# Splitting the weights of two projections ahead of their use, in the feed-forward layers, and loading them back as parts

## The chip, the cores and the metric

The kernel runs on one core of a Trainium2 chip. TensorE (PE) multiplies, VectorE (DVE), ScalarE (ACT) and GpSimd (POOL) do the element-wise work, and SyncE (SP) issues nearly all DMAs, in order, on one queue that the core's 16 DMA engines serve. The metric is the device time of one execution in microseconds (us).

## What is computed

Two decoder blocks, one after the other, on 512 tokens of width 1024, in fp32. Cut to the order of the large products:

```python
# first block
h = h + s5_mixer(rmsnorm(h), ...)            # ends in y @ w_glu
h = h + square(relu(rmsnorm(h) @ w_up[0])) @ w_down[0]
h = h + sigmoid(rmsnorm(h) @ w_ple_gate[0]) * (p[0] @ w_ple_proj[0])
k, v = rope((rmsnorm(h) * kv_norm) @ w_k), (rmsnorm(h) * kv_norm) @ w_v
h = h + window_attention(rope(rmsnorm(h) * norm_mix @ w_q), k, v) @ w_o
h = h + square(relu(rmsnorm(h) @ w_up[1])) @ w_down[1]
h = h + sigmoid(rmsnorm(h) @ w_ple_gate[1]) * (p[1] @ w_ple_proj[1])
# second block: a scan layer, then a differential attention
z, x, B, C, dt = split(rms_norm(h) @ a_w_in)  # 6144 + 32 columns
x, B, C = silu(causal_conv(x, B, C))          # 4 taps
x = h + (norm(scan(x, dt, B, C) * silu(z)) @ a_w_out)
...
```

A product keeps fp32 accuracy with three passes: each operand is split exactly into a high and a low part (hi = the value rounded to the multiplier's format, lo = the rest), and hi·hi, hi·lo and lo·hi are added in PSUM.

## The kernel before

`plan` (L665) lists all weight matrices in their order of use. `Weights` (L62 to L119) streams them. A unit is one DMA of 1 MB (a few are smaller) from DRAM into one of three `raw` buffers (`load_to`, L84). A chunk of eight 128-row K tiles by 128 columns, 1024 elements per partition, is then split (`split_to`, L92): for weights with a norm's gain GpSimd multiplies the raw chunk by it in place (L100); ScalarE copies it, rounded, to `whi` (L103); VectorE or GpSimd subtracts to get `wlo` (L104). There are four `whi` and four `wlo` buffers, and `take` (L115) asks for the split two chunks ahead of the use. `lo_eng` chooses who subtracts: GpSimd in the first attention (L1135) and in the scan layer (L1398), VectorE elsewhere.

`gemm` (L721) makes one output tile of 128 features by 512 tokens at a time: 24 products for each chunk of eight K tiles (`three`, L211). The stages, in the order of time: the first mixer, `glu` (L858), the first feed-forward layer (`mlp`, L886), the gated side input (`ple`, L966), `first_attention` (L983), the second `mlp` and `ple`, `mamba` (the scan layer, L1168), `second_attention`. In `mlp` each half has 16 tiles up (`up`, L901: relu and square on ScalarE, the square once more on GpSimd, the low part on VectorE) and 8 tiles down of 16 K tiles each (`down`, L911).

In `mamba` eight groups of four tiles (B, C and two of x) and 16 gate tiles z run through `gemm`. Between them the convolution `conv` (L1262, three multiply-adds on VectorE), and the scan `ssd` (L1277) as a generator whose steps are put behind the tiles: decays `dec` are loaded by DMA from the DRAM row `acs` (L1325), get an offset on VectorE (L184), an exponential on ScalarE and a mask on GpSimd (L174).

What runs in which order on each engine is set by a scheduler that is given the program and its dependencies; within an engine, and in SP's queue, the order is then fixed, and an instruction that waits holds up those behind it.

Of the kernel before, what the change touches and what calls it, by code (L numbers as in the profile page):

```python
# [62 lines left out]
class Weights:  # L63
    """Streams the weight matrices in their order of use: DRAM -> raw fp32 -> exact (hi, lo) f32r pairs."""

    def __init__(self, nc, raw_pool, hl_pool, ahead_dma, ahead_split):
        self.nc, self.raw_pool, self.hl_pool = nc, raw_pool, hl_pool
        self.units, self.chunks = [], []
        self.loaded, self.split, self.used = 0, 0, 0
        self.ahead_dma, self.ahead_split = ahead_dma, ahead_split  # L70
        self.raw, self.hl = {}, {}
        self.lo_eng = nc.vector

    def add(self, w, k0, kt, c0, cols, cut=128, kg=8, gain=None):
# [3 lines left out]
        self.units.append((w[k0:k0 + 128 * kt, c0:c0 + cols].rearrange("(k p) n -> p k n", p=128), kt, cols))  # L78
        gain = None if gain is None else (gain, k0 // 128)
        new = [(u, k, min(kg, kt - k), c, min(cut, cols - c), gain) for c in range(0, cols, cut) for k in range(0, kt, kg)]  # L80
        self.chunks.extend(new)
        return new

    def load_to(self, u):  # L84
        while self.loaded < min(u, len(self.units)):
            ap, kt, cols = self.units[self.loaded]
# [5 lines left out]
    def split_to(self, n):  # L92
        while self.split < min(n, len(self.chunks)):
            u, k, kn, c, cn, gain = self.chunks[self.split]
            self.load_to(u + self.ahead_dma)
            src = self.raw[u][:, k:k + kn, c:c + cn]
# [11 lines left out]
    def borrow(self, shape):  # L108
        """One of the raw buffers for something else, until its last use."""
# [12 lines left out]
class Builder:  # L122
    #: the order of the queries' and gates' tiles in the second attention
    QG = (0, 1, 8, 2, 9, 3, 10, 4, 11, 5, 12, 6, 13, 7, 14, 15)
    #: the number of the queries' tiles before the values in the first attention
    V_AT = 2
    #: the groups after whose tensors the gates of groups 0, 1, ... come; those of the other groups come last
# [72 lines left out]
    def pair(self, src, g=None, name="x"):  # L200
        """src (fp32) -> exact f32r pair of src * g."""
# [14 lines left out]
    def dexp(self, out, x, n, pool):  # L216
        t = lambda nm: pool.tile([128, n], F32, tag="ex" + nm, name="ex" + nm)  # noqa: E731
# [15 lines left out]
    def dsincos(self, so, co, x, n, pool):  # L233
        t = lambda nm: pool.tile([128, n], F32, tag="sc" + nm, name="sc" + nm, bufs=1)  # noqa: E731
# [44 lines left out]
    def s5(self, extra):  # L279
        """extra: steps of work for TensorE that needs nothing of this."""  # L280
        nc, ins, tc = self.nc, self.ins, self.tc
        V, A, G = self.V, self.A, self.G
        with ExitStack() as cx:
            sm = cx.enter_context(tc.tile_pool(name="s5s", bufs=1))
            s2 = cx.enter_context(tc.tile_pool(name="s5t", bufs=2))
            small = lambda nm, n=32: sm.tile([128, n], F32, name=nm)  # noqa: E731
# [12 lines left out]
            b3 = lambda t: t.rearrange("p (r h) -> p r h", h=16)  # noqa: E731  # L299
# [15 lines left out]
            # tiles whose other blocks stay zero, for every other four pairs of groups  # L315
            two = lambda nm, sh: [sm.tile(sh, F32, name=f"{nm}{i}") for i in range(2)]  # noqa: E731
# [21 lines left out]
            # discretisation  # L338
# [75 lines left out]
            # powers of the phase of a  # L414
# [12 lines left out]
            # 1 / rms of the tokens  # L427
# [7 lines left out]
            # C, states on partitions  # L435
# [10 lines left out]
            # g*d over the channels  # L446
# [1263 lines left out]
```

## Time and profile before

| what | value |
|---|---|
| median of three runs | 2049.87 us (2049.61 to 2052.82) |
| span of the profiled execution, first to last instruction | 2043.2 us |
| what the median run takes beyond that span | 6.7 us |
| PE busy | 1919.8 us (94%) |
| DVE, ACT, POOL busy | 1271.6, 922.7, 640.8 us |
| read from HBM, written | 166.00 MB, 2.16 MB |

The page gives the profiled execution by its span alone; the runs' times lie 6.4 to 9.6 us above it. Busy time is that of instructions; issuing a DMA, waiting and branching are not counted. PEclk is the clock that TensorE was granted as a share of its full 2.4 GHz (1.00 is 2.4, half is 1.2). A row of the chain of waits gives what the chain's end was waiting for in that stretch. Records of matmuls overlap, since they are pipelined: their pace is read from how many start in a stretch.

### The profile page before, as it was taken

The page shows a single profiled execution, that of the slowest core. Times are in us where ns is not written, and L with a number is a line of the kernel's source. Part 1 is how long each engine was busy: PE and PEld are TensorE (multiplying, and loading weights), DVE is VectorE, ACT ScalarE, POOL GpSimd, SP SyncE. Part 2 cuts the span into 40 slices and gives each one's busy share as a digit, 9 for nine tenths or more (in the row PEclk, how much of TensorE's full clock was granted, in tenths as well). Part 3 has the DMA queues.
Part 4 walks back from the last instruction along what each step waited for, and adds up shares of the span by engine and source line. Part 5 has one row for each costly group of instructions (what it writes and reads, how often), then busy time and mean ns, then how long its engine had stood idle before and what let it go on. Part 6 is the DMA issues. An engine that isn't in the chain of part 4 may idle for free.

```text
span 2043.2 us, 25227 instructions
## 1 busy us (share of the span) xinstructions
PE 1919.8 (94%) x9482; PEld 1581.2 (77%) x9482; DVE 1271.6 (62%) x2042; ACT 922.7 (45%) x1590; POOL 640.8 (31%) x415
## 2 busy tenths in 40 slices
PE   3799999999999899999999999988989899999998
PEld 1688888888887787888888886766867678887888
DVE  8995543333448685633333457988888764727885
ACT  5644333223334376442233335456656643434553
POOL 7500122012117720231022117456655543432000
PEclk9899999999999899999999999988999899999999
DMA  5003323323322431333323313232323223425331
GB/s 137 6 7 117 103 83 103 102 85 102 103 95 81 125 95 53 96 91 103 102 85 101 103 54 105 69 98 88 98 72 103 87 74 117 119 88 138 111 93 42
DMA packets 232059, 185.78 MB, mean 91 GB/s; under 512 B 22611, under 2 KB 213790, under 8 KB 231938
## 3 DMA queue, kind: packets, MB, share of 16 engines
q1 hardware_dynamic: 219072, 179.43, 29.8%
q10 hardware_dynamic: 12866, 4.75, 0.9%
q8 instruction: 75, 1.23, 0.2%
q14 instruction: 46, 0.38, 0.1%
HBM read 166.00 MB, written 2.16 MB: 82 GB/s over the span
## 4 chain that ended last, share of the span: by engine, by line
PE 68%; DVE 18%; ACT 5%; issue 4%; POOL 2%; DMA 2%; SPq 0%; ACTq 0%; DVEq 0%; POOLq 0%
PE pg L190 62%; DVE cy L177 3%; DVE lent L171 2%; DVE dec L184 1%; PE pm L190 1%; PE sc L190 1%; ACT L187 1%; DVE wlo L104 1%; DVE pr L182 1%; ACT whi L103 1%; DMA dec<-acs 1%; DVE h L171 1%; PE po L190 1%; DVE xl L177 1%; PE o L190 1%
## 5 line engine op out<-in xcount | busy, mean ns | idle before, releaser
L103 ACT ACTIVATE whi<-raw 128x1024 fp32r<-128x1024 f32 x289 | 304.4, 1055 | 691.7 <-PE pg L190 601.7
L190 PE MATMUL pg<-xh,whi 128*128 128x512 f32 x1424 | 567.7, 399 | 8.3 <-ACT xh L187 4.8
L190 PE MATMUL pg<-xl,whi 128*128 128x512 f32 x1424 | 563.3, 396 | 2.2 <-DVE xl L171 2.2
L190 PE MATMUL pg<-xh,wlo 128*128 128x512 f32 x1424 | 562.7, 395 | 0.0
L104 DVE TENSOR_TENSOR wlo<-raw,whi 128x1024 fp32r<-128x1024 f32 (+1 forms) x229 | 300.3, 1314 | 367.7 <-ACT whi L103 367.5
L190 PEld LDWEIGHTS pg<-xh,whi 128*128 128x128 f32 x1424 | 271.1, 190 | 68.5 <-ACT xh L187 5.6
L190 PEld LDWEIGHTS pg<-xl,whi 128*128 128x128 f32 x1424 | 271.3, 191 | 62.9 <-DVE xl L171 4.5
L190 PEld LDWEIGHTS pg<-xh,wlo 128*128 128x128 f32 x1424 | 271.0, 190 | 57.3 <-issue 1.6
L174 POOL TENSOR_TENSOR b<-a 128x512 f32<-128x512 f32 x64 | 98.9, 1545 | 438.2 <-ACT a L187 418.7
L190 PE MATMUL pg<-hh,whi 128*128 128x512 f32 x512 | 199.2, 389 | 0.0
L190 PE MATMUL pg<-hl,whi 128*128 128x512 f32 x512 | 199.2, 389 | 0.0
L190 PE MATMUL pg<-hh,wlo 128*128 128x512 f32 x512 | 199.2, 389 | 0.0
L104 POOL TENSOR_TENSOR wlo<-raw,whi 128x1024 fp32r<-128x1024 f32 x60 | 157.2, 2623 | 110.0 <-ACT whi L103 109.5
L171 POOL TENSOR_TENSOR acc<-acc,sq 128x512 f32<-128x512 f32 x48 | 75.9, 1588 | 314.6 <-ACT sq L187 276.3
L100 POOL TENSOR_TENSOR raw<-raw,gv 128x1024 f32<-128x1024 f32 x44 | 93.6, 2146 | 139.8 <-DMA raw<-in_b_w_in_dram 54.8
L177 DVE SCALAR_TENSOR_TENSOR cy<-cx,cw,cy 128x511 f32<-128x511 f32 (+2 forms) x96 | 107.4, 1134 | 9.5 <-ACT cy L187 9.1
L190 PEld LDWEIGHTS pg<-hh,wlo 128*128 128x128 f32 x512 | 96.1, 188 | 20.0
L190 PEld LDWEIGHTS pg<-hh,whi 128*128 128x128 f32 x512 | 96.1, 188 | 20.0
L190 PEld LDWEIGHTS pg<-hl,whi 128*128 128x128 f32 x512 | 96.1, 188 | 19.9
L171 DVE TENSOR_TENSOR t<-pg,r 128x512 f32<-128x512 f32 x48 | 32.7, 688 | 107.5 <-PE pg L190 107.4
L187 ACT ACT_TABLE_LOAD x61 | 78.3, 1283 | 34.4 <-DVE cy L177 19.4
L171 DVE TENSOR_TENSOR hl<-b,hh 128x512 fp32r<-128x512 f32 x64 | 44.2, 691 | 56.9 <-POOL b L174 56.9
(409 smaller groups left out, 3132.8 us busy)
## 6 DMA issues: line engine op xcount, KB each, us to landing
raw<-in_w_up_dram SPq DMA_DIRECT2D x32, 1024.0 KB
raw<-in_w_down_dram SPq DMA_DIRECT2D x32, 1024.0 KB
raw<-in_a_w_in_dram SPq DMA_DIRECT2D x16, 1024.0 KB
raw<-in_ssm_w_glu_dram SPq DMA_DIRECT2D x8, 1024.0 KB
raw<-in_w_ple_gate_dram SPq DMA_DIRECT2D x8, 1024.0 KB
raw<-in_a_w_in_dram SPq DMA_DIRECT2D x16, 512.0 KB
dec<-acs SPq DMA_DIRECT2D x32, 256.0 KB
raw<-in_a_w_out_dram SPq DMA_DIRECT2D x8, 1024.0 KB
```

The costliest lines, as they stand in the source:

```text
L100: self.nc.gpsimd.tensor_tensor(out=src, in0=src, in1=g, op=MUL)
L103: self.nc.scalar.activation(out=hi, in_=src, func=ACTF.Copy)
L104: self.lo_eng.tensor_tensor(out=lo, in0=src, in1=hi.bitcast(F32), op=SUB)
L171: (eng or self.V).tensor_tensor(out=out, in0=a, in1=b, op=op)
L174: self.G.tensor_tensor(out=out, in0=a, in1=b, op=op)
L177: self.V.scalar_tensor_tensor(out=out, in0=a, scalar=s, in1=b, op0=op0, op1=op1)
L182: eng.tensor_scalar(out=out, in0=a, scalar1=s1, scalar2=None, op0=op0)
L184: eng.tensor_scalar(out=out, in0=a, scalar1=s1, scalar2=s2, op0=op0, op1=op1)
L187: self.A.activation(out=out, in_=in_, func=func, **kw)
L190: self.T.matmul(out=out, lhsT=lhsT, rhs=rhs, start=start, stop=stop)
```

## The change

The weights `w_k`, `w_v` and `w_q` of the first attention (12 chunks) and all columns of `a_w_in` in the scan layer but the 32 of dt (48 chunks) are marked `early`. They have no unit in the `raw` buffers any more. Their split is done in half chunks (512 elements per partition), one in each `up` tile of the two feed-forward layers and two in each `down` tile of them (but for the last two of the second half): 60 in each layer, 120 in all. A step stores the two parts of the half chunk before the last in DRAM, loads the next raw half chunk, and splits the one that was loaded a step ago: the gain (first attention's only) on GpSimd, the high part on ScalarE, the low part on VectorE in place. Raw halves have two buffers and high parts two. At the place of use `split_to` now issues two DMAs, of 512 KB each, from DRAM into `whi` and `wlo`; nothing is split there.

```diff
+    def early_step(self, more=True):
+
+        nc, pool = self.nc, self.early_pool
+        if self.done:
+            (chunk, h), raw, hi = self.done
...
+            nc.sync.dma_start(out=self.kept[chunk][h, 0], in_=hi.bitcast(F32))
+            nc.sync.dma_start(out=self.kept[chunk][h, 1], in_=raw)
+            self.done = None
+        was, self.came = self.came, None
+        if more and self.n_early < len(self.early):
...
+            raw = pool.tile([128, 512], F32, tag="eraw", name="eraw", bufs=2)
+            nc.sync.dma_start(out=raw.rearrange("p (k n) -> p k n", k=n),
+                              in_=self.units[u][0][:, k + h * n:k + h * n + n, c:c + cn])
+            self.came = (chunk, h), raw
+        if was:
...
+                nc.gpsimd.tensor_tensor(out=x, in0=x, in1=g, op=MUL)
+            hi = pool.tile([128, 512], F32R, tag="ehi", name="ehi", bufs=2)
+            nc.scalar.activation(out=hi, in_=raw, func=ACTF.Copy)
+            nc.vector.tensor_tensor(out=raw.bitcast(F32R), in0=raw, in1=hi.bitcast(F32), op=SUB)
+            self.done = (*was, hi)
...
     def split_to(self, n):
...
+            if self.units[u][3]:
+                hi = self.hl_pool.tile([128, kn, cn], F32R, tag="whi", name="whi")
+                lo = self.hl_pool.tile([128, kn, cn], F32R, tag="wlo", name="wlo")
+                for i, t in enumerate((hi, lo)):
+                    self.nc.sync.dma_start(out=t.rearrange("p k n -> p (k n)").bitcast(F32).rearrange("p (h n) -> p h n", h=2),
+                                           in_=self.kept[chunk][:, i].rearrange("h p n -> p h n"))
...
             def up(m, ps):
...
+                self.W.early_step()
...
             def down(m, ps):
...
+                    if m == 6:
+                        self.W.early_end()
+                if hf == 0 or m < 6:
+                    for _ in range(2):
+                        self.W.early_step()
```

In `plan` the units of `w_k`, `w_v`, `w_q` and of `a_w_in` (but the first, of 32 columns) get `early=True`. The line numbers of the kernel after are higher by 57 to 67 than those of before.

GpSimd in the scan layer, over one group's scan; `wlo` are the low parts of weights, `dec` the decays, `cy` the tensors of the group. Before:

```order
L174 TENSOR_TENSOR dec_10640<-dec_10640,cb_10556 128x512
L174 TENSOR_TENSOR dec_10641<-dec_10641,cb_10556 128x512
L104 TENSOR_TENSOR wlo<-raw,whi 128x1024
L174 TENSOR_TENSOR dec_10714<-dec_10714,cb_10556 128x512
L174 TENSOR_TENSOR dec_10715<-dec_10715,cb_10556 128x512
L104 TENSOR_TENSOR wlo<-raw,whi 128x1024 x2
L174 TENSOR_TENSOR cy_9987<-cy_9987,r_10503 128x512
L174 TENSOR_TENSOR cy_10059<-cy_10059,r_10503 128x512
```

The same engine and place after:

```order
L231 TENSOR_TENSOR dec_11520<-dec_11520,cb_11436 128x512
L231 TENSOR_TENSOR dec_11521<-dec_11521,cb_11436 128x512
L231 TENSOR_TENSOR dec_11592<-dec_11592,cb_11436 128x512
L231 TENSOR_TENSOR dec_11593<-dec_11593,cb_11436 128x512
L231 TENSOR_TENSOR cy_10881<-cy_10881,r_11385 128x512
L231 TENSOR_TENSOR cy_10953<-cy_10953,r_11385 128x512
```

The subtractions between the scan's own instructions are gone from GpSimd, all 48 of them in this layer.

ScalarE in the tiles up of the first feed-forward layer (`a` is the relu of a tile, `hh` its square). Before:

```order
L187 ACTIVATE hh_2800<-a_2798 128x512
L103 ACTIVATE whi<-raw 128x1024
L187 ACTIVATE a_2835<-pg 128x512
L187 ACTIVATE hh_2837<-a_2835 128x512
L103 ACTIVATE whi<-raw 128x1024
```

After, where `ehi` is the high part of an early half chunk and `eraw` what its DMA brought:

```order
L160 ACTIVATE whi<-raw 128x1024
L244 ACTIVATE a_2795<-pg 128x512
L120 ACTIVATE ehi<-eraw 128x512 x2
L244 ACTIVATE hh_2797<-a_2795 128x512
L160 ACTIVATE whi<-raw 128x1024
L244 ACTIVATE a_2840<-pg 128x512
L244 ACTIVATE hh_2842<-a_2840 128x512
L120 ACTIVATE ehi<-eraw 128x512
```

The scheduler took the early splits ahead of where the program has them: the 60 of the first layer stand between the 10th and the 60th split of a streamed chunk in ScalarE's order (from `glu` on, 50 tiles in all), those of the second between the 95th and the 140th (45 tiles, from the product with `w_o` on).

SP's queue in the first feed-forward layer, tiles down: before, `raw<-in_w_down_dram` stands there eight times in a row. After:

```order
L136 DMA raw<-in_w_down_dram 128x16x128
L108 DMA eraw<-in_a_w_in_dram 128x4x128
L99 DMA kept_3723<-eraw 128x512
L98 DMA kept_3814<-ehi 128x512
L108 DMA eraw<-in_a_w_in_dram 128x4x128
L99 DMA kept_3814<-eraw 128x512
L108 DMA eraw<-in_a_w_in_dram 128x4x128
L98 DMA kept_3814<-ehi 128x512
L136 DMA raw<-in_w_down_dram 128x16x128
```

Between two loads of streamed weights there are now about seven DMAs of 256 KB each; each store waits for ScalarE or VectorE, and each load of `eraw` for the landing of the store that frees its buffer.

## Rows read from the trace of the kernel before

**Rows 1.** The page: busy time by engine, and the chain's shares by engine.

```profile
PE 1919.8 (94%) x9482; PEld 1581.2 (77%) x9482; DVE 1271.6 (62%) x2042; ACT 922.7 (45%) x1590; POOL 640.8 (31%) x415
...
PE 68%; DVE 18%; ACT 5%; issue 4%; POOL 2%; DMA 2%; SPq 0%; ACTq 0%; DVEq 0%; POOLq 0%
```

**Rows 2.** Busy time by stretch: length, engines (instructions), PEclk, DMA share, GB/s.

```profile
200.00:610.00 410.00, 410.00 (x1808) 339.12 (x1808) 168.27 (x170) 135.76 (x174) 66.63 (x45) 1.00 0.33 99
650.00:700.00 50.00, 41.09 (x193) 32.66 (x192) 40.35 (x28) 18.06 (x27) 41.18 (x21) 0.90 0.27 81
700.00:810.00 110.00, 106.79 (x718) 88.61 (x718) 78.52 (x194) 80.12 (x228) 24.71 (x13) 1.00 0.35 99
860.00:1190.00 330.00, 330.00 (x1455) 272.88 (x1455) 128.41 (x131) 107.71 (x137) 57.05 (x37) 1.00 0.33 96
1250.00:1650.00 400.00, 358.31 (x1789) 287.00 (x1790) 325.00 (x455) 233.54 (x300) 229.04 (x127) 0.93 0.29 89
```

**Rows 3.** Groups by line, 300 to 600 us: busy, mean ns, idle before, releaser.

```profile
L104 DVE TENSOR_TENSOR wlo<-raw,whi 128x1024 fp32r<-128x1024 f32 x56 | 68.5, 1223 | 113.3 <-ACT whi L103 113.3
L103 ACT ACTIVATE whi<-raw 128x1024 fp32r<-128x1024 f32 x55 | 58.4, 1061 | 199.6 <-PE pg L190 186.8 <-issue 12.8
...
L171 DVE TENSOR_TENSOR hl<-b,hh 128x512 fp32r<-128x512 f32 x26 | 18.0, 693 | 24.2 <-POOL b L174 24.2
L187 ACT ACTIVATE hh<-a 128x512 fp32r<-128x512 f32 x26 | 16.5, 633 | 1.3
```

**Rows 4.** Groups by line on DVE, 1250 to 1650 us.

```profile
L184 DVE TENSOR_SCALAR dec<-dec,tok 128x128 f32<-128x128 f32 x128 | 50.8, 458 | 8.6 <-ACT ea L187 7.7 <-issue 0.8
L177 DVE SCALAR_TENSOR_TENSOR cy<-cx,cw,cy 128x509 f32<-128x509 f32 x32 | 41.3, 1296 | 0.2
L177 DVE SCALAR_TENSOR_TENSOR cy<-cx,cw,cy 128x510 f32<-128x510 f32 x32 | 37.8, 1185 | 0.2
L177 DVE SCALAR_TENSOR_TENSOR cy<-cx,cw,cy 128x511 f32<-128x511 f32 x32 | 29.3, 919 | 9.1 <-ACT cy L187 9.1
...
L177 DVE SCALAR_TENSOR_TENSOR xl<-cy,gv,xh 128x512 fp32r<-128x512 f32 x10 | 13.0, 1310 | 8.1 <-ACT xh L187 8.1
```

**Rows 5.** The tiles dec and cy on DVE, same stretch: ns min/median/max.

```profile
L184 DVE TENSOR_SCALAR dec<-dec,tok x128: 269/279/2423, 1339.8 to 1623.5; 128x128 f32<-128x128 f32 x128
...
L177 DVE SCALAR_TENSOR_TENSOR cy<-cx,cw,cy x96: 654/745/2940, 1276.9 to 1606.4; 128x511 f32<-128x511 f32 x32, 128x510 f32<-128x510 f32 x32, 128x509 f32<-128x509 f32 x32
L177 DVE SCALAR_TENSOR_TENSOR cy<-cy,dsk,yd x16: 735/740/750, 1357.2 to 1637.3; 128x512 f32<-128x512 f32 x16
L177 DVE SCALAR_TENSOR_TENSOR xl<-cy,gv,xh x10: 739/999/2358, 1397.2 to 1564.3; 128x512 fp32r<-128x512 f32 x10
```

**Rows 6.** Groups by line on POOL, 1250 to 1650 us.

```profile
L104 POOL TENSOR_TENSOR wlo<-raw,whi 128x1024 fp32r<-128x1024 f32 x48 | 126.8, 2643 | 98.3 <-ACT whi L103 97.8 <-PE pg L190 0.5
L174 POOL TENSOR_TENSOR dec<-dec,cb 128x512 f32<-128x512 f32 x32 | 45.5, 1437 | 34.7 <-ACT dec L187 30.4 <-DVE cb L171 4.2
L174 POOL TENSOR_TENSOR cy<-cy,z 128x512 f32<-128x512 f32 x15 | 22.0, 1470 | 2.8 <-ACT z L187 2.3
L174 POOL TENSOR_TENSOR cy<-cy,ea 128x384 f32<-128x384 f32 x16 | 18.4, 1153 | 24.1 <-DVE ea L171 23.8
L174 POOL TENSOR_TENSOR cy<-cy,r 128x512 f32<-128x512 f32 x10 | 13.8, 1406 | 6.8 <-DVE r L790 6.8
```

**Rows 7.** The chain of waits, 640 to 692 us: start, us, what.

```profile
658.43 5.18 POOL raw L100 x2
...
679.90 2.90 DVE cosT L171
```

**Rows 8.** The chain of waits in the scan layer: two of its DMAs.

```profile
1355.41 7.59 DMA dec<-acs
...
1560.91 3.11 DMA dec<-acs
```

**Rows 9.** What SP's queue waited for: us in total, times, longest.

```profile
SPq L1325 <- DMA acs<-dt: 2.6, 1, 2.6
```

More of the change, by code (lines that the diff above doesn't have):

```diff
@@ L72, in __init__, with add @@
         self.lo_eng = nc.vector
-    def add(self, w, k0, kt, c0, cols, cut=128, kg=8, gain=None):
+        self.early, self.kept, self.n_early, self.came, self.done = [], {}, 0, None, None
+    def add(self, w, k0, kt, c0, cols, cut=128, kg=8, gain=None, early=False):
         u = len(self.units)
-        self.units.append((w[k0:k0 + 128 * kt, c0:c0 + cols].rearrange("(k p) n -> p k n", p=128), kt, cols))
+        self.units.append((w[k0:k0 + 128 * kt, c0:c0 + cols].rearrange("(k p) n -> p k n", p=128), kt, cols, early))
         gain = None if gain is None else (gain, k0 // 128)
@@ L81, in add, with keep, early_end @@
         self.chunks.extend(new)
-        return new
+        if early:
+            self.early.extend((x, h) for x in new for h in range(2))
+        return new
+    def keep(self, pool, dram):
+        self.early_pool, self.dram = pool, dram
+    def early_step(self, more=True):
+        nc, pool = self.nc, self.early_pool
+        if self.done:
+            (chunk, h), raw, hi = self.done
+            if chunk not in self.kept:
+                self.kept[chunk] = self.dram.tile([2, 2, 128, 512], F32, name=f"kept{len(self.kept)}")
+            nc.sync.dma_start(out=self.kept[chunk][h, 0], in_=hi.bitcast(F32))
[3 more added lines that the diff above has]
+        if more and self.n_early < len(self.early):
+            chunk, h = self.early[self.n_early]
+            self.n_early += 1
+            u, k, kn, c, cn, _ = chunk
+            n = kn // 2
+            raw = pool.tile([128, 512], F32, tag="eraw", name="eraw", bufs=2)
[3 more added lines that the diff above has]
+        if was:
+            ((u, k, kn, c, cn, gain), h), raw = was
+            if gain is not None:
+                n = kn // 2
+                o = self.gcol[gain[0]] + gain[1] + k + h * n
+                g = self.gains[:, o:o + n].unsqueeze(2).to_broadcast([128, n, cn])
+                x = raw.rearrange("p (k n) -> p k n", k=n)
+                nc.gpsimd.tensor_tensor(out=x, in0=x, in1=g, op=MUL)
[3 more added lines that the diff above has]
+            self.done = (*was, hi)
+    def early_end(self):
+        while self.done or self.came:
+            self.early_step(False)
     def load_to(self, u):
         while self.loaded < min(u, len(self.units)):
-            ap, kt, cols = self.units[self.loaded]
+            ap, kt, cols, early = self.units[self.loaded]
+            if early:
+                self.loaded += 1
+                continue
             t = self.raw_pool.tile([128, kt, cols], F32, tag="raw", name="raw")
@@ L93, in split_to @@
         while self.split < min(n, len(self.chunks)):
-            u, k, kn, c, cn, gain = self.chunks[self.split]
+            u, k, kn, c, cn, gain = chunk = self.chunks[self.split]
             self.load_to(u + self.ahead_dma)
+            if self.units[u][3]:
[4 more added lines that the diff above has]
+                                           in_=self.kept[chunk][:, i].rearrange("h p n -> p h n"))
+                self.hl[self.split] = (hi, lo)
+                self.split += 1
+                continue
             src = self.raw[u][:, k:k + kn, c:c + cn]
@@ L674, in plan @@
         self.plan_mlp_gate(0)
[L675 removed]
+        W.add(ins["w_k"], 0, 8, 0, 256, gain="kv", early=True)
         for m in range(0, 8, 2):
             if m == self.V_AT:
[L678 to L679 removed]
+                W.add(ins["w_v"], 0, 8, 0, 256, cut=256, kg=4, gain="kv", early=True)
+            W.add(ins["w_q"][0], 0, 8, m * 128, 256, gain="mix1", early=True)
         W.add(ins["w_ple_proj"][1], 0, 2, 0, D, cut=512)
@@ L927, in mlp @@
         self.drop(r2[0])
+        cx.close()
         return out, acc2
```

16 lines of the change are left out of this document (8 added, 8 removed).

## The prediction, made before the changed kernel ran

> **What bounds the kernel now.** I read the page first [rows 1]: PE is busy for 94% of the span and 68% of the chain that ended last, so only a stage in which PE waits can give much. The table by stretch [rows 2] says which stages these are. From 200 to 610 us and from 860 to 1190 us (`glu` and the two feed-forward layers) PE is busy in every microsecond at the full clock, and DVE, ACT and POOL have half their time or more left; a tile of 24 products takes 24 x 410 / 1808 = 5.44 us there. In the first attention (650 to 810 us) PE idles 8.9 + 3.2 us, and the granted clock of 0.90 in its first 50 us means 10 us at half speed, thus 5 us of work lost: 17 us in all. In the scan layer (1250 to 1650 us) PE idles 41.7 us, and the clock of 0.93 costs 0.07 x 400 = 28 us: 70 us in all. These 87 us are the most that the change can win. What PE waits for in the scan layer is mostly DVE, busy 325 of 400 us, with ACT at 234 and POOL at 229 beside it.
>
> **What leaves the scan layer.** POOL loses 48 subtractions of 2643 ns [rows 6], 127 of its 229 us. ACT loses 48 copies of 1061 ns [rows 3], 51 us. DVE loses no instruction, but much waiting: its multiply-adds of the convolution have a median of 745 ns and means of 919, 1185 and 1296 ns, with single ones of 2940 ns; the decays' offsets have a median of 279 ns and a mean of 458 ns [rows 4, 5]. The form that reads PSUM for one of its inputs (`cy<-cy,dsk,yd`) never leaves 735 to 750 ns. The long ones take about one POOL instruction more than the short ones. Over the medians this is 108.4 - 96 x 0.745 = 36.9 us for the convolution, 128 x 0.179 = 22.9 us for the decays, and 13.0 - 10 x 0.739 = 5.6 us for `xl` over its least: 65 us of DVE's 325. How much of it is due to the subtractions? If a DVE instruction that starts while POOL works waits for the rest of POOL's instruction, the share goes by count times the square of the duration: 335 for `wlo` and 66, 32, 21 and 20 for the other four [rows 6], 71%. By busy time alone it would be 127 of 229, 55%. The longest DVE instructions, 2.1 to 2.2 us over the median, exceed the mean of every other group of POOL there by half and more [rows 5, 6], which speaks for the first: 0.7 x 65 = 45 us. The Trainium skill has this as a rule (SBUF — State Buffer, "SBUF: two separate sides"): DVE and GpSimd share one pair of ports as an exclusive lock for a whole instruction, and the loser fully blocks. By it 45 us would come free, by a shared bandwidth 36 us; the trace agrees with the lock.
>
> So DVE falls from 325 to 280 us, ACT to 183, POOL to 102, for PE work of 400 - 70 = 330 us. DVE was late, then PE is. Not all 70 us come back: the chain dt, softplus, decays is serial, the same two engines still hand work to each other in a fixed order at 85% load of DVE, and the decays' DMAs now queue behind twice the bytes: 48 MB of parts instead of 24 MB. One decay load took 7.59 us behind other loads, one 3.11 us without [rows 8]; 16 pairs of loads that meet a 1 MB load 0.2 times more often lose 16 x 0.2 x 4.5 = 14 us at most if all stood on the chain, and nothing if none did. I take two thirds of the 70 us, which is also what DVE is freed of: **-45 us** (bounds -70 and -20).
>
> **What leaves the first attention.** Its 12 gains, 12 copies and 12 subtractions go. Between 658 and 666 us the chain is two gains of 2.6 us in front of the products that feed the residual, and later the product with the cosines takes 2.90 us on DVE beside POOL [rows 7], where like ones take 0.69 us [rows 3]. That is 5.2 + 2.2 = 7.4 us, and the half clock that follows such waits is 5 us [rows 2]: **-12 us** of the 17 (bounds -17 and -4).
>
> **What comes into the feed-forward layers.** Per half chunk ACT gets a copy of 0.633 us and DVE a subtraction of 0.693 us [rows 3], 60 of each a layer: 38 us of ACT, 42 us of DVE, beside 108 to 136 and 128 to 168 us in stretches of 330 to 410 us [rows 2]. They hide behind PE. 24 gains on POOL (half of 2.6 us each, 31 us) fall into `glu` and the first tiles up, where POOL is busy 67 of 410 us. What may not hide is the chain from half to half, because ACT works in order and the copy waits for a DMA. With two buffers each pair of halves takes one turn: load, copy, subtract, store, and the next load into the freed buffer. No row shows a store of 256 KB; SP waited 2.6 us for one of 64 KB [rows 9], and a load of 256 KB took 3.11 us [rows 8]. I take 2.6 us for the store at the low end and 3.1 us at the high end. A turn then takes 3.1 + 0.63 + 0.69 + 2.6 = 7.0 us when nothing is in its way. A streamed weight of 1.05 MB occupies the DMA engines for 1.05 MB / (99 GB/s / 0.33) = 3.5 us [rows 2], once every two tiles (10.9 us). High end: each turn meets it in full, 3.1 + 0.63 + 0.69 + 3.1 + 3.5 = 11.0 us. A turn of 7 us meets one in 64% of cases, and its two transfers find half of it left on average, 0.64 x 3.5 = 2.2 us; thus 9.2 us, and I take **9 us**.
>
> ACT's order leaves the turns less: 30 turns stand among 50 tiles in the first layer, 272 us or 9.1 us each, and among 45 tiles in the second, 245 us or 8.2 us each. Behind a late copy on ACT wait the splits of the streamed weights. These have slack: with four buffers a split may start when the chunk four before it is done, three tiles (16.3 us) before its use, and takes 1.06 + 1.22 us [rows 3], so 14 us of lateness cost nothing; ACT shows this slack as 187 us of waiting for PE in 300 us [rows 3]. At 9 us a turn the first layer loses nothing; the second is late by 270 - 245 = 25 us, and loses 25 - 14 = 11 us: **+11 us**. At 7.0 us it is 0; at 11.0 us 330 - 272 - 14 = 44 and 330 - 245 - 14 = 71, together +115 us. SP is also moved past: its streamed loads queue behind stores, but a raw buffer is asked for five tiles before its split, 27 us, of which the load takes 3.5 us of transfer and about 2.2 us around it (3.11 us less the 0.9 us that 256 KB take at that rate); this slack is larger than ACT's.
>
> The loads of parts in the attention and the scan layer, two of 512 KB for each tile, ask for 1.05 MB in 5.44 us, 193 GB/s of the 300; they start three tiles ahead and take 5.7 us by the same working, so they hide. If that cover failed, a tile would take 5.7 us and not 5.44, 0.3 us for each of 60 chunks, 16 us.
>
> **The sum.** -45 - 12 + 11 = -46 us against the span of 2043.2 us: 1997 us. The median of the runs is 6.7 us above the span, so 2004 us.
>
> **The rivals.** (1) *The parts' chain becomes the bound of the feed-forward layers*, and the kernel is slower. Place: ACT's `ehi` before the splits and the relu. It decides once a turn takes over 10 us: the loss is then 60 x 10 - 517 - 28 = 55 us and eats the gain of 57. At 11.0 us the kernel would take 2043 - 57 + 115 + 7 = 2108 us. For it speaks that the queue is one for all, and in-order waits on ACT, DVE and SP that I priced at nothing; against it, that engines which run late have no other waits left. The Trainium skill (DMA: Bandwidth & Descriptors, "Latency and other measured facts") gives the memory's access latency as 0.2 us on average and 2 us at high load. Were that added to both transfers of a turn, it would last 3.6 us longer, 12.6 us, and the kernel would take some 2200 us; no row here shows the queue at a high load. (2) *The scan layer stays bound by its serial chains* (convolution, decays, table loads): only 20 us there and 4 us in the attention come back, with +11 in the second feed-forward layer: 2043 - 24 + 11 + 7 = 2037 us. For it speaks that DVE keeps 280 us of work there; against it, that a sixth of its time was waiting. (3) *All comes back*: 2043 - 87 + 7 = 1963 us, if turns take under 8 us. (4) *Nothing happens*: what PE waits for was never the weights' work, and the turns hide: 2050 us. Against it stand the chain's two gains and the long DVE instructions.
>
> **How the numbers follow.** Forecast as above (1975 to 2025 us) 0.60; rival 1 0.13, rival 2 0.15, rival 3 0.07, rival 4 0.05. 0.2%, 4 us, is about what a measurement of this kernel can tell from no change. Faster: 0.60 + 0.15 + 0.07 = 0.82; the same 0.05; slower 0.13. The range of eight in ten leaves out most of rival 1 above 2055 us and the lowest end: 1966 to 2055 us.
>
> **What would show it.** In the scan layer: means of the convolution's multiply-adds near 0.8 us, POOL near 102 us, PE idle and half-clock time under 30 us, the stretch about 355 us long. In the first attention: no gain in the chain. In the feed-forward layers: PE busy throughout at full clock in the first; in the second some 11 us of gaps that end with ACT's `whi`, and turns of the `eraw` buffers near 9 us. Wrong it would be by a turn over 10 us (gaps of PE in both layers, ACT waiting for DMAs of `eraw`), or by PE in the scan layer waiting as long as before, for `dec` DMAs or the scan's DVE chain.

## The result and the profile after

The changed kernel takes 2106.51 us in the median (2104.62 to 2108.53) beside 2049.89 us for the kernel before (2049.61 to 2052.82): a ratio of 1.0275 (1.0263 to 1.0287), 2.8% slower. The span of the profiled execution is 2102.8 us, 59.6 us more than before. The forecast of 2004 us and its range missed it; rival 1, 2108 us at turns of 11.0 us, comes within 2 us of it. One execution of `pinned` below and one of the kernel before took 4.89 ms; the medians leave them out.

The page after, answering to [rows 1]: busy time, HBM traffic, and the chain's shares by engine and by line.

```profile
PE 1942.2 (92%) x9482; PEld 1589.4 (76%) x9482; DVE 1282.7 (61%) x2156; ACT 926.2 (44%) x1650; POOL 494.9 (24%) x373
...
HBM read 228.91 MB, written 65.08 MB: 140 GB/s over the span
...
PE 45%; DMA 17%; DVE 8%; ACT 5%; issue 3%; SPq 2%; POOL 1%; ACTq 0%; DVEq 0%; POOLq 0%
PE pg L247 39%; DMA kept<-eraw 8%; DMA eraw<-in_a_w_in_dram 7%; PE sc L247 1%; ACT ehi L120 1%; DVE wlo L161 1%; DVE eraw L121 1%; ACT L244 1%; DMA dec<-acs 1%; DVE cy L234 1%; DVE dec L241 1%; PE yd L247 1%; PE po L247 1%; PE yo L247 1%; D
```

DMAs were 2% of the chain and are 17% now; 8% of the span are stores `kept<-eraw`, 7% loads of `eraw`. The same stretches as in [rows 2] (the second feed-forward layer and the scan layer begin later, and the windows are cut anew to them, so that they hold other numbers of products), with the same columns:

```profile
200.00:610.00 410.00, 374.90 (x1569) 302.66 (x1568) 196.88 (x209) 148.27 (x214) 84.59 (x62) 0.95 0.65 202
860.00:1230.00 370.00, 337.68 (x1413) 270.06 (x1412) 169.46 (x186) 136.20 (x197) 57.96 (x38) 0.95 0.67 205
1330.00:1710.00 380.00, 366.97 (x1904) 296.80 (x1903) 291.08 (x473) 204.18 (x278) 131.79 (x94) 0.99 0.50 164
```

PE, which lost nothing in the first two stretches before, now idles 35.1 and 32.3 us there, and the clock of 0.95 costs 0.05 x 410 = 20.5 and 0.05 x 370 = 18.5 us more: 106 us. In the scan layer PE idles 13.0 us, not 41.7, and has nearly its full clock back (0.99, not 0.93). So both halves of the story happened: the gain, and a larger loss.

What ScalarE waits for, over the whole span (us in total, times, longest), and its early copies in the first and in the second feed-forward layer:

```profile
ACT ehi L120 <- DMA eraw<-in_a_w_in_dram: 271.3, 57, 9.1
...
ACT ehi L120 <- POOL eraw L118: 59.6, 19, 7.0
```

```profile
L120 ACT ACTIVATE ehi<-eraw 128x512 fp32r<-128x512 f32 x60 | 37.7, 630 | 198.4 <-DMA eraw<-in_a_w_in_dram 108.3 <-POOL eraw L118 59.6 <-issue 24.9
...
L120 ACT ACTIVATE ehi<-eraw 128x512 fp32r<-128x512 f32 x60 | 37.7, 630 | 197.2 <-DMA eraw<-in_a_w_in_dram 163.0 <-issue 22.6 <-DVE wlo L161 11.4
```

Nearly 200 us of waiting in each layer stand in front of copies that take 38 us. One turn shows how. SP's queue (start, duration of the issue, line, DMA), then ScalarE and PE in the same stretch:

```profile
446.40 0.38 SPq L136 DMA_DIRECT2D raw<-in_w_up_dram  x1
446.88 0.79 SPq L99 DMA_DIRECT2D kept<-eraw  x1
449.35 0.32 SPq L98 DMA_DIRECT2D kept<-ehi  x1
450.08 0.90 SPq L99 DMA_DIRECT2D kept<-eraw  x1
456.41 1.64 SPq L108 DMA_DIRECT2D eraw<-in_a_w_in_dram  x2
```

```profile
448.69 0.63 ACT L120 ACTIVATE ehi<-eraw 128x512 fp32r<-128x512 f32 x1 [3.23 <-DMA eraw<-in_a_w_in_dram]
449.23 1.04 ACT L160 ACTIVATE whi<-raw 128x1024 fp32r<-128x1024 f32 x1
459.34 0.63 ACT L120 ACTIVATE ehi<-eraw 128x512 fp32r<-128x512 f32 x1 [9.07 <-DMA eraw<-in_a_w_in_dram]
459.88 1.04 ACT L160 ACTIVATE whi<-raw 128x1024 fp32r<-128x1024 f32 x1
```

```profile
456.52 0.39 PE L247 MATMUL pg<-hh,wlo 128*128 128x512 f32 x1
460.97 0.80 PE L247 MATMUL pg<-hh,whi 128*128 128x512 f32 x1 [4.07 <-ACT whi L160]
```

The stores at 446.88 and 450.08 share the DMA engines with the 1 MB weight issued just ahead of them. The loads into their buffers, next in SP's queue, can start only when they have landed, 9.5 us after the first store and 7.6 us after the second (the row's second load starts at 457.66). The copy comes at 459.34, the streamed chunk's split, behind it in ScalarE's order, at 459.88, and PE has stood for 4 us. Its products then run at half clock (0.80 and 0.63 us where they took 0.39).

From first to last copy the 60 halves take 335 us in the first layer and 319 us in the second: 5.7 and 5.4 us each, a turn of 11.4 and 10.8 us where the prediction took 9.

### The profile page after: what moved, and what is told of

It is laid out like the page before. It is cut to its first block, busy times and chain, and to the rows that moved or that the text cites. A ratio compares the mean times of both kernels' runs of the same rounds, so it can differ in the third digit from the quotient of the medians.

```text
span 2102.8 us, 26183 instructions
## 1 busy us (share of the span) xinstructions
PE 1942.2 (92%) x9482; PEld 1589.4 (76%) x9482; DVE 1282.7 (61%) x2156; ACT 926.2 (44%) x1650; POOL 494.9 (24%) x373
## 4 chain that ended last, share of the span: by engine, by line
PE 45%; DMA 17%; DVE 8%; ACT 5%; issue 3%; SPq 2%; POOL 1%; ACTq 0%; DVEq 0%; POOLq 0%
PE pg L247 39%; DMA kept<-eraw 8%; DMA eraw<-in_a_w_in_dram 7%; PE sc L247 1%; ACT ehi L120 1%; DVE wlo L161 1%; DVE eraw L121 1%; ACT L244 1%; DMA dec<-acs 1%; DVE cy L234 1%; DVE dec L241 1%; PE yd L247 1%; PE po L247 1%; PE yo L247 1%; DVE h L228 0%
## 5 line engine op out<-in xcount | busy, mean ns | idle before, releaser
L161 DVE TENSOR_TENSOR wlo<-raw,whi 128x1024 fp32r<-128x1024 f32 (+1 forms) x223 | 295.1, 1325 | 176.5 <-ACT whi L160 169.8
L160 ACT ACTIVATE whi<-raw 128x1024 fp32r<-128x1024 f32 (+1 forms) x229 | 239.7, 1050 | 314.6 <-PE pg L247 248.6
L121 DVE TENSOR_TENSOR eraw<-eraw,ehi 128x512 fp32r<-128x512 f32 x120 | 95.7, 799 | 319.2 <-ACT ehi L120 318.8
L120 ACT ACTIVATE ehi<-eraw 128x512 fp32r<-128x512 f32 x120 | 75.4, 630 | 395.7 <-DMA eraw<-in_a_w_in_dram 271.3
L247 PE MATMUL pg<-hh,whi 128*128 128x512 f32 x512 | 205.8, 402 | 28.7 <-ACT hh L244 14.3
L247 PE MATMUL pg<-hh,wlo 128*128 128x512 f32 x512 | 205.4, 401 | 3.8 <-DVE wlo L161 3.8
L247 PE MATMUL pg<-hl,whi 128*128 128x512 f32 x512 | 204.8, 400 | 2.2 <-DVE hl L228 2.2
L157 POOL TENSOR_TENSOR raw<-raw,gv 128x1024 f32<-128x1024 f32 x32 | 65.4, 2065 | 127.0 <-DMA raw<-in_b_w_in_dram 45.2
L234 DVE SCALAR_TENSOR_TENSOR cy<-cx,cw,cy 128x510 f32<-128x510 f32 (+2 forms) x96 | 83.6, 879 | 8.2 <-ACT cy L244 7.7
```

What stands on the lines that cost most here:

```text
L120: nc.scalar.activation(out=hi, in_=raw, func=ACTF.Copy)
L121: nc.vector.tensor_tensor(out=raw.bitcast(F32R), in0=raw, in1=hi.bitcast(F32), op=SUB)
L157: self.nc.gpsimd.tensor_tensor(out=src, in0=src, in1=g, op=MUL)
L160: self.nc.scalar.activation(out=hi, in_=src, func=ACTF.Copy)
L161: self.lo_eng.tensor_tensor(out=lo, in0=src, in1=hi.bitcast(F32), op=SUB)
L234: self.V.scalar_tensor_tensor(out=out, in0=a, scalar=s, in1=b, op0=op0, op1=op1)
```

## The experiments

Below, "room" is what ScalarE's order gives the halves of a layer: the splits of streamed chunks between the first and the last early copy, times 5.44 us a tile. "Late" is what the halves took beyond it. "Stretch" is how much later than before PE's last tile up of the second feed-forward layer is evacuated (1113.3 us after the start before), which counts what both layers lose.

| kernel | median us | halves, first / second layer: splits | took, us | late, us | stretch, us |
|---|---|---|---|---|---|
| changed | 2106.5 | 50 / 45 | 335 / 319 | 63 / 74 | 105.8 |
| gain_alone | 2000.1 | – | – | – | -0.4 |
| cost_alone | 2159.5 | 50 / 45 | 335 / 322 | 63 / 77 | 116.5 |
| no_stores | 2017.5 | 31 / 28 | 187 / 172 | 18 / 19 | 20.8 |
| three | 2040.8 | 40 / 37 | 256 / 237 | 39 / 35 | 45.0 |
| scan_only (60 + 36 halves) | 2077.7 | 48 / 26 | 305 / 190 | 44 / 49 | 76.5 |
| scan_three (60 + 36) | 2038.3 | 40 / 21 | 241 / 144 | 23 / 30 | 37.0 |
| stores_pool | 2017.1 | 58 / 55 | 329 / 316 | 13 / 17 | 22.8 |
| pinned | 2064.0 | 60 / 60 | 365 / 359 | 38 / 33 | 62.2 |
| pinned_three | 2036.6 | 60 / 60 | 351 / 351 | 25 / 25 | 38.9 |
| pairs | 2024.4 | 58 / 58 | 336 / 327 | 20 / 12 | 26.7 |
| pinned_pool | 2000.5 | 60 / 60 | 330 / 328 | 4 / 2 | 5.7 |

**Gain and cost apart.** `gain_alone` splits only the first chunk ahead and loads its parts everywhere; `cost_alone` does all early work and does not use it.

```diff
-        if more and self.n_early < len(self.early):
+        if more and self.n_early < 2:
...
-                                           in_=self.kept[chunk][:, i].rearrange("h p n -> p h n"))
+                                           in_=self.kept[self.early[0][0]][:, i].rearrange("h p n -> p h n"))
```

> The gain alone: only the first early chunk is split in the feed-forward layer and stored, and every place of use loads that one chunk's parts (so the values of the other 59 chunks are left out). My theory, that the use side gained what was forecast and the feed-forward layers lost all that came back: -57 us against before, 1990 to 1997 us, the feed-forward layers without gaps, the scan layer's products as in the changed kernel. Rival, that the loads of the parts themselves cost time in the scan layer and the attention: 2030 us or more.

```diff
-        self.units.append((w[k0:k0 + 128 * kt, c0:c0 + cols].rearrange("(k p) n -> p k n", p=128), kt, cols, early))
+        self.units.append((w[k0:k0 + 128 * kt, c0:c0 + cols].rearrange("(k p) n -> p k n", p=128), kt, cols, False))
```

> The cost alone: all 120 early steps run and store their parts, but the products load and split their weights at the place of use as before, so the stored parts are never read. My theory: the feed-forward layers lose as in the changed kernel, 105 to 115 us over before, 2155 to 2165 us, and the scan layer and the attention take their old times. Rival, that the feed-forward layers lose because of what the scan's loads ask for later or earlier in the queue: under 2100 us.

Measured: 2000.08 us (ratio 0.976, 0.971 to 0.980) and 2159.48 us (1.054, 1.049 to 1.059). -48 and +111 us beside the kernel before, run with them (2048.0 us), make +63, where the change itself gave +57: the two add up to within 7 us. The first lies 3 us above the range that I expected, the second inside it. The gain lies in the scan layer alone: the feed-forward stretches of `gain_alone` show PE busy for 410.0 of 410 and 330.0 of 330 us at a clock of 1.00, and from the end of the tiles up to the end of the kernel it needs 46.3 us less than before.

**What holds a turn.** `no_stores` drops the stores of all chunks but the first; `three` has a third raw buffer.

```diff
+        if self.done and self.done[0][0] != self.early[0][0]:
+            self.done = None
         if self.done:
```

> The changed kernel, but only the first chunk's parts are stored; the other 118 early halves are loaded, copied and subtracted and then dropped, and every place of use loads the first chunk's parts (values of the other 59 chunks are left out). Theory 1, a buffer is held by its stores, which land late behind a streamed weight: a turn falls from 11.4 us to 5 or 6 us, the feed-forward layers have no gaps, 1990 to 2000 us. Theory 2, the copies and subtractions themselves, in ScalarE's and VectorE's fixed order, hold up the splits: 2070 us or more.

```diff
-            raw = pool.tile([128, 512], F32, tag="eraw", name="eraw", bufs=2)
+            raw = pool.tile([128, 512], F32, tag="eraw", name="eraw", bufs=3)
```

> The changed kernel with three eraw buffers in place of two (a 640-byte constant of the scan layer moves to a pool of its own to make room). Theory 1, the latency of a turn is the bound: three buffers in 11.4 us are 3.8 us a half, less than the 4.1 to 4.5 us that a half has, so most of the loss of 110 us goes: 1995 to 2025 us. Theory 2, the DMA engines are at the limit of what they move while weights, loads and stores share them: it stays within 15 us of 2106 us.

Measured: 2017.54 us (0.984, 0.980 to 0.989) and 2040.84 us (0.996, 0.995 to 0.997); both lie between the ranges of the two theories. A half falls from 5.7 to 3.2 us without stores and to 4.3 us with three buffers. So the stores hold the buffers, as theory 1 has it, and the DMA engines were not at their limit. But neither kernel got all back, and the table shows where it went: the order of these kernels has the halves closer together (31 and 40 splits in the first layer), and again more closely than they run. That the scheduler reckons with shorter turns than the chip gives is a reading; its times are not on record. Every kernel whose copies are not held (`pinned` below holds them) is late by 13 to 77 us a layer, whatever a half costs.

**Fewer halves.** `scan_only` leaves the first attention's weights as they were; `scan_three` does so with three buffers.

```diff
-        W.add(ins["w_k"], 0, 8, 0, 256, gain="kv", early=True)
+        W.add(ins["w_k"], 0, 8, 0, 256, gain="kv")
```

> Only the scan layer's 48 chunks are split ahead, 48 halves a layer in place of 60; the first attention's weights are split at their use as before. My theory, that the attention gains nothing (its stretch took 228 us before and 228 us with parts loaded) and the loss goes with the number of halves beyond what fits: at 5.7 us a half the first layer has room for 48 (272 us), the second for 43 of 48 (245 us); with the waits at the ends of stages some 25 us are lost and 46 gained: 2015 to 2045 us. Rival, every half costs the same 0.9 us of 110 us for 120: 2049 - 46 + 86 = 2090 us.

> The scan layer's 48 chunks only, with three eraw buffers. Both theories of the turn expect less loss than with 60 halves a layer: the three-buffer kernel lost 41 us in the feed-forward layers at 4.1 us a half, most of it where a stage ends. If that loss is due to the first attention's halves (their gain on GpSimd, in glu and the first tiles up), it falls to under 15 us: 2003 to 2015 us. If it is due to the order at the ends of stages, whatever the halves are: 2025 to 2045 us.

Measured: 2077.69 us (1.014, 1.011 to 1.017) and 2038.25 us (0.995). My expectation for the first fell. One error was plain: a step stands in each tile, so the layers do 60 and 36 halves and not 48 each. The other is the table's: the 36 halves of the second layer are packed into 26 splits and late by 49 us. `scan_three` lies where it should if the order makes the loss. Neither the count of the halves nor the first attention's gains on GpSimd set the loss alone: without those gains the first layer's 60 halves take 305 us and not 335, but `scan_three` still loses 37.0 us where `three` lost 45.0.

**Order and queue.** `stores_pool` issues both stores from GpSimd. `pinned` holds each early copy behind what the program has ahead of it on ScalarE. `pinned_three` and `pinned_pool` combine these.

```diff
-            nc.sync.dma_start(out=self.kept[chunk][h, 0], in_=hi.bitcast(F32))
-            nc.sync.dma_start(out=self.kept[chunk][h, 1], in_=raw)
+            nc.gpsimd.dma_start(out=self.kept[chunk][h, 0], in_=hi.bitcast(F32))
+            nc.gpsimd.dma_start(out=self.kept[chunk][h, 1], in_=raw)
```

> The changed kernel, with the two stores of a half issued by GpSimd, in its own DMA queue, and two eraw buffers as in the change. Theory A, the stores land late (7.5 us in place of 2.0) because they stand behind a 1 MB weight in one queue: they now land in 2 to 3.5 us, the turn falls from 11.4 us to 8 or 9 us, 2000 to 2040 us. Theory B, the transfers share the 16 DMA engines whatever their queue: stores still land in 5 to 8 us while a weight is under way, and the time stays above 2075 us. A third way, GpSimd's order now holds the stores behind its squares and the squares behind the stores' waits: PE waits for hl, above 2110 us.

```diff
-            nc.scalar.activation(out=hi, in_=raw, func=ACTF.Copy)
+            self.tc.keep_in_program_order(nc.scalar.activation(out=hi, in_=raw, func=ACTF.Copy))
```

> The changed kernel, two buffers and stores in SP's queue as in the change, but each early copy on ScalarE is held behind the instructions that the program has ahead of it, so that the 60 halves of a layer stand among 60 splits of streamed chunks and not among 50 and 45. Theory, the loss is the time that the halves take less the products that the order puts between the first and the last of them (before: 335 - 50 x 5.44 = 63 us and 319 - 45 x 5.44 = 74 us): 60 x 5.44 = 326 us stand against 60 x 5.6 = 336 us, so some 10 us a layer are lost at most, 2000 to 2020 us. Rival, the stores behind the weights hold up the splits wherever the copies stand: above 2060 us.

> The same with three eraw buffers. By the theory of the order a half may take 5.44 us and needs 4.1 us with three buffers: no loss in the feed-forward layers, 1998 to 2006 us. If what is left of the loss is contention of the transfers, it stays as with two buffers, 2010 to 2020 us.

> Two buffers, copies held in the program's order, stores issued by GpSimd in its own queue. With the unheld copies this queue gave 2017 us while a half still took 5.5 us: its order had 58 and 55 splits among the halves, not 50 and 45. If that order and not the queue was the reason, this kernel takes the same time as the held one with stores in SP's queue, within 6 us. If the queue itself helps, it is faster by more.

Measured: `stores_pool` 2017.08 us (0.985, 0.982 to 0.987), `pinned` 2064.0 us (1.008, 1.006 to 1.011), `pinned_three` 2036.61 us (0.994), `pinned_pool` 2000.52 us (0.977, 0.975 to 0.979). `pinned` missed its 2000 to 2020 us and has its rival's time, above 2060 us; whether it has the rival's cause, `pairs` below tests. `pinned_three` lies above both of its ranges. `stores_pool` has the time of theory A but not its turn: a half still takes 5.6 and 5.4 us, and its stores land no sooner by much. Its time goes with its order, which leaves 58 and 55 splits where the changed kernel has 50 and 45. The page's rows on its stores (size, median us from issue to landing):

```profile
kept<-ehi POOLq DMA_DIRECT2D x120, 256.0 KB, 4.7
kept<-eraw POOLq DMA_DIRECT2D x120, 256.0 KB, 4.5
```

In the changed kernel the stores of low parts land after 5.0 us in the median and 9.8 at most, a store with nothing beside it after 2.0. Those with a weight under way beside them take 5.8 us in the median there and 4.8 us in `stores_pool`, those with none 3.3 and 2.8 us. So the queue a store stands in does not make it late: what else is under way does (theory B). The Trainium skill (DMA: Bandwidth & Descriptors, "Issuing engines are not separate DMA queues") says so: DMAs from different engines run on the same 16 DMA engines, and issuing from several saves only the time to issue them. On the landing the runs agree. On the kernel's time they do not: with the copies held in the same way, `pinned_pool` takes 63 us less than `pinned`. Most of what was saved is waiting in order. From the end of its subtraction to the issue of its store a low part waits 2.0 and 2.4 us in `pinned` (means of the two layers) and 0.5 us in `pinned_pool`, while the store then lands after 5.0 and 4.8 us in one and 4.6 us in the other. SP's queue in `pinned`:

```profile
522.10 0.38 SPq L108 DMA_DIRECT2D eraw<-in_a_w_in_dram  x1
522.53 0.50 SPq L98 DMA_DIRECT2D kept<-ehi  x1
523.14 0.36 SPq L99 DMA_DIRECT2D kept<-eraw  x1
526.39 0.38 SPq L108 DMA_DIRECT2D eraw<-in_a_w_in_dram  x1
526.82 0.51 SPq L136 DMA_DIRECT2D raw<-in_w_down_dram  x1
527.42 1.87 SPq L98 DMA_DIRECT2D kept<-ehi  x1
529.40 0.37 SPq L99 DMA_DIRECT2D kept<-eraw  x1
534.54 0.38 SPq L108 DMA_DIRECT2D eraw<-in_a_w_in_dram  x1
```

Each load waits for the landing of the store just ahead of it (523.14 to 526.39, 529.40 to 534.54), and the other buffer's stores cannot be issued before that load: the two buffers' stores follow each other, 12.4 us for two halves. A third buffer makes the halves little faster there (351 us). That was a reading still; `pairs` tested it with one queue. Every second step stores two halves, then loads two, then splits two.

```diff
-        if more and self.n_early < len(self.early):
+        for _ in range(2):
+            if not (more and self.n_early < len(self.early)):
+                break
...
+        self.calls += 1
+        if more and self.calls % 2:
+            return
```

> Two buffers, stores in SP's queue, copies held in the program's order, but the halves are worked on in pairs: four stores, then two loads, then two copies and two subtractions, in every second tile. With single halves and held copies the kernel lost 63 us, at 6.1 us a half. Theory, SP's queue is in order, and a load that waits for the landing of one buffer's store holds back the stores of the other buffer, so the two buffers' stores follow each other: in pairs they overlap, a half takes 5.4 to 5.6 us, 2005 to 2030 us. Rival, the stores are late because the 1 MB weights stand ahead of them in the same queue: 2055 us or more, as with single halves.

Measured: 2024.35 us (0.988, 0.986 to 0.990), 5.7 and 5.5 us a half, 40 us less than `pinned` with the same queue, buffers, weights and bytes, and as many DMAs to issue: these 40 us are not issue time, and the rival (2055 us or more) fell. A low part waits 0.7 and 0.8 us for the issue of its store. The 18 to 24 us between `pairs` and `pinned_pool` were not taken apart. Its queue has the stores of both buffers together:

```profile
531.29 1.00 SPq L113 DMA_DIRECT2D eraw<-in_a_w_in_dram  x2
532.33 0.51 SPq L141 DMA_DIRECT2D raw<-in_w_down_dram  x1
535.00 2.33 SPq L101 DMA_DIRECT2D kept<-ehi  x2
537.43 0.98 SPq L102 DMA_DIRECT2D kept<-eraw  x2
542.71 1.03 SPq L113 DMA_DIRECT2D eraw<-in_a_w_in_dram  x2
```

In `pinned_pool` the feed-forward layers are nearly whole again, at twice the DMA share of [rows 2]:

```profile
200.00:610.00 410.00, 407.54 (x1790) 336.68 (x1789) 215.93 (x231) 167.12 (x233) 154.05 (x187) 1.00 0.66 212
860.00:1190.00 330.00, 330.00 (x1456) 272.88 (x1455) 168.92 (x188) 141.32 (x196) 119.47 (x154) 1.00 0.74 234
```

**The scan layer's gain.** `pool_busy` is `gain_alone` with a GpSimd subtraction put back for each chunk, into a tile that nobody reads.

```diff
+                if self.junk is not None:
+                    self.nc.gpsimd.tensor_tensor(out=self.junk, in0=self.junk, in1=hi.bitcast(F32), op=SUB)
                 self.hl[self.split] = (hi, lo)
```

> The gain alone, as before (one chunk split and stored, every use loads its parts; values of the other chunks left out), but in the scan layer GpSimd does one subtraction of 128x1024 for each chunk into a spare tile, which reads the loaded high part. Theory, DVE's and GpSimd's shared port makes both slow and this was the scan layer's loss: 35 to 45 of the 46 us come back, 2035 to 2045 us, with the convolution's multiply-adds at a mean over 1.1 us again. Rival, what came free was ScalarE's 51 us of copies and the handing over of the splits: under 2012 us.

Measured: 2062.29 us (1.007, 1.004 to 1.009), all of the gain and 14 us more, above the 2035 to 2045 us that I expected; where the 14 us come from was not traced. VectorE's convolution and decays in the scan layer, in the changed kernel and then in `pool_busy`, and GpSimd's subtraction there; first the convolution before, whose forms [rows 4] has apart, beside 458 ns for the decays there:

```profile
L177 DVE SCALAR_TENSOR_TENSOR cy<-cx,cw,cy 128x511 f32<-128x511 f32 (+2 forms) x96 | 107.4, 1134 | 9.5 <-ACT cy L187 9.1
```

```profile
L234 DVE SCALAR_TENSOR_TENSOR cy<-cx,cw,cy 128x510 f32<-128x510 f32 (+2 forms) x96 | 83.6, 879 | 8.2 <-ACT cy L244 7.7
L241 DVE TENSOR_SCALAR dec<-dec,tok 128x128 f32<-128x128 f32 x128 | 37.4, 354 | 17.4 <-ACT ea L244 17.4
```

```profile
L237 DVE SCALAR_TENSOR_TENSOR cy<-cx,cw,cy 128x510 f32<-128x510 f32 (+2 forms) x96 | 112.1, 1182 | 4.6 <-ACT cy L247 4.1
L244 DVE TENSOR_SCALAR dec<-dec,tok 128x128 f32<-128x128 f32 x128 | 59.3, 529 | 8.5 <-ACT ea L247 8.2
...
L152 POOL TENSOR_TENSOR junk<-junk,whi 128x1024 f32<-128x1024 f32 x47 | 127.7, 2716 | 85.2 <-DMA whi<-kept 72.1 <-PE xt L253 12.7
```

VectorE's instructions are the same in both; only GpSimd works beside them. The rival, ScalarE's 51 us of copies, is out: they stay away in `pool_busy`. How a slow instruction comes about shows in the trace of before. Of the 128 decays 24 last over 0.3 us, and each of them ends 0.08 us after an instruction of GpSimd; of the 96 multiply-adds 34 last over 0.78 us, and each of them ends 0.54 to 0.55 us after one. So a slow one has waited for the end of an instruction of GpSimd, whichever that was. One pair from before:

```profile
1598.97 2.52 POOL L104 TENSOR_TENSOR wlo<-raw,whi 128x1024 fp32r<-128x1024 f32 x1
1599.21 2.83 DVE L177 SCALAR_TENSOR_TENSOR cy<-cx,cw,cy 128x509 f32<-128x509 f32 x1
```

This is the Trainium skill's lock (SBUF — State Buffer, "SBUF: two separate sides"), and the trace agrees.

**The first attention.** `best_attq` is `pinned_pool`, `pinned_three_attq` is `pinned_three`, each with the first attention's parts loaded through GpSimd's queue. `best_scan` is `pinned_pool` without early work for the attention; `pinned_pool_2` is a repeat.

```diff
-                    self.nc.sync.dma_start(out=t.rearrange("p k n -> p (k n)").bitcast(F32).rearrange("p (h n) -> p h n", h=2),
+                    (self.nc.sync if gain is None else self.nc.gpsimd).dma_start(out=t.rearrange("p k n -> p (k n)").bitcast(F32).rearrange("p (h n) -> p h n", h=2),
```

> Three buffers and copies held in order, and the first attention's parts are loaded through GpSimd's queue in place of SP's. Theory, the attention gained nothing because a load of parts stood behind some twenty small DMAs of 0.65 us each in SP's queue and PE waited 4.6 us for it, with the half clock after it: 3 to 8 us faster than the kernel with three buffers and held copies. Rival, what bounds the attention is the chain of its norm and rotation, as before: the same within 3 us.

> The same, with the first attention's parts loaded through GpSimd's queue. If PE's single wait of 4 us for a part behind SP's small DMAs and the half clock after it are what the attention lost of its gain, 3 to 6 us less: 1994 to 1998 us. If GpSimd's own work delays the loads as much, the same within 2 us.

> Held copies, stores issued by GpSimd, and only the scan layer's 48 chunks split ahead. The first attention's parts gained 0.4 us in the kernel that had the gain alone, so nothing is lost by leaving them: 1997 to 2003 us. If they do gain the 12 us that were forecast: 2008 us or more.

> The kernel with held copies and stores issued by GpSimd once more, with more runs, beside the two below: 1998 to 2003 us.

Measured, in this order: 2033.36, 2001.51 (0.977, 0.975 to 0.979), 2003.35 (0.978, 0.976 to 0.980) and 2005.94 us (0.979, 0.976 to 0.982). `best_attq` did not reach its 1994 to 1998 us, and the last two lie 0.4 and 2.9 us above what I expected. From the last relu of the first feed-forward layer to the first of the second it is 337.5 us before, 336.5 in `gain_alone`, 338.3 in `best_scan` and 332.9 in `best_attq`. In `gain_alone` SP's queue shows what ate the attention's gain, and PE's list of waits what it cost:

```profile
693.57 0.62 SPq L1079 DMA_DIRECT2D turned<-ry  x1
694.24 0.62 SPq L1080 DMA_DIRECT2D turned<-ry  x1
694.96 0.39 SPq L148 DMA_DIRECT2D whi<-kept  x1
695.45 0.41 SPq L148 DMA_DIRECT2D wlo<-kept  x1
```

```profile
PE pg L247 <- DMA whi<-kept: 4.4, 1, 4.4
```

Some twenty small DMAs of 0.65 us stand ahead of the parts. Through the other queue that wait is gone and some 4 us come back; in the whole time this is within what the repeats differ by. `best_attq`, `best_scan` and `pinned_pool` cannot be told apart; all three beat both kernels.

## Why the prediction was wrong

- **The failed step: the turn.** 9 us were taken, between 7.0 and 11.0; it is 11.4 and 10.8 us. Followed from copy to copy (means of the two layers in the changed kernel's trace), the copy takes 0.63 us, the subtraction 0.8, the store of the low part 4.9 and 4.8 from issue to landing, the next load 3.65, and 1.5 and 1.1 us are waits between these steps: 11.5 and 10.9 us in all. The prediction had 0.63, 0.69, 2.6 and 3.1 us, and 2.2 us more for the weights that store and load meet. Two of its terms were too small. The store takes 4.9 us for 2.6, 5.8 in the median and up to 9.8 where it meets a weight, because both stores of a half, the other buffer's stores and the weight are under way together; but the 2.2 us cover most of that, and store and load together are 0.6 us over. The waits between the steps I had priced at nothing, and named that in rival 1; they are the larger part of what was missing. In the first layer the gain on GpSimd also stands in the chain and was left out of the turn: ScalarE waited 59.6 us for it. That a load which waits in SP's queue holds the stores behind it, as `pinned` shows, is only 0.4 us of a turn in the changed kernel.
- **The formula came close here.** Room of 272 and 245 us and a slack of 14 us a layer: with the measured durations it gives 335 - 272 - 14 = 49 and 319 - 245 - 14 = 60, 109 us where 105.8 were lost. It is within 5 us in `cost_alone` and `three` as well, but 6 to 20 us short in the other eight kernels of the table with early work: the slack is not there in full in them, and why was not traced. The loss was known for a turn; the turn was not. A low end and a high end of 0 and +115 us should have said that a turn built on one unmeasured store decides the sign. A chance of 0.13 for rival 1 was too low, since nothing in the trace of before showed a store under load. That its 2108 us came so near is in part luck: its loss of 115 us was 105.8, its gain of 57 us was 46.
- **The longer turn of rival 1.** The Trainium skill's latency (DMA: Bandwidth & Descriptors, "Latency and other measured facts") made it 12.6 us a turn, which was too much. The extra does not stand on each transfer: a load of `eraw` lands after 3.1 us in the median, a store beside nothing after 2.0 us.
- **Scan layer, -45 us: right in size.** 46.3 us came. VectorE was freed of 23.8 us (convolution, 107.4 to 83.6), 13.4 us (decays, 50.8 to 37.4) and 5.0 us (`xl`, 13.0 to 8.0): 42 of the 65 us of waiting, 65%, between the 71% of a lock and the 55% of a shared bandwidth; when the slow instructions end decides for the lock. The multiply-adds have a mean of 0.88 us and not 0.8. That two thirds of PE's 70 us would come back was a choice, and so the nearness of -45 is in part luck. The cause, GpSimd's instructions, is shown by `pool_busy`. Rival 2 fell.
- **First attention, -12 us: wrong.** 1 us came. The gains left the chain as forecast; the loads of parts took their place, issued late behind small DMAs. "They start three tiles ahead" counted buffers and not the queue. 4.6 us come with another queue; PE's longest waits there are then 2.9 us for the small DMAs of `qs` and 2.6 us for the rotation's `rx`. What became of the rest was not tried.
- **Parts' loads, nothing: right in the scan layer** (`gain_alone` moves 164 GB/s there, and PE's waits for parts are one of 4.4 us, in the attention).

## What to carry to other kernels

Work that hides in an engine's free time still has to fit the order in which that engine takes it: count the instructions of the bound stream between the first and the last added one, and compare with what the added chain takes by measured transfers under the new load, with the waits between its steps. A load that waits for a store should not stand in one in-order queue with the next buffer's stores; issue the stores elsewhere, or all stores ahead of all loads. If a scheduler puts the added work closer together than it runs, hold the added instructions to the pace of the stream that they ride on: here this and the queue together turned +57 us into -43 to -49.

## What the runs showed that was not expected

- A 256 KB store lands after 2.0 us alone and beside a 1 MB load after up to 9.8 us from SP's queue and 8.1 us from GpSimd's (5.0 and 4.5 us in the median of all stores of low parts), while the DMA engines are 65 to 74% busy.
- A single gap of PE of 4 us is followed by 3.4 to 6.8 us at half clock; of 106 us lost in the feed-forward layers 39 are clock and not idle time.
- Fewer early halves (`scan_only`, 76.5 us) and faster ones (`three` 45.0, `no_stores` 20.8) still lost, since the order was packed more closely for them.
